# Down projection of a ConvFFN in fp32: the second block group takes six gated tiles in place of four, the plain group between the two takes two in place of four, and three of the seven low parts of its operands move from VectorE to GpSimd

## The chip, the cores and the metric

The kernel runs on one core of a Trainium2 chip. The metric is the device time of one execution in microseconds (us); less is better. Beside the time of several runs there is one execution recorded by the hardware profiler, from which all rows below come.

Six engines appear in the rows. PE (TensorE) multiplies matrices, and PEld is its weight load, which runs beside it. DVE (VectorE) and POOL (GpSimd) do elementwise work, ACT (ScalarE) copies and casts, and SP (SyncE) issues DMA transfers, as POOL does too. Each engine works through its own queue in order and waits for the others by semaphores.

## The reference

The reference is a trunk of two layers over 16 learned meta tokens and 1024 frames (1040 rows) with a model width of 1024. Each layer has a mixing part (gated linear attention and softmax attention) and then a feed-forward part, which is the one that the change touches:

```python
def conv_ffn(x, w_up, conv_w, conv_b, w_down):
    h = x @ w_up
    L = h.shape[1]
    hp = jnp.pad(h, ((0, 0), (CONV_W - 1, 0), (0, 0)))
    hc = conv_b
    for j in range(CONV_W):
        hc = hc + hp[:, j:j + L] * conv_w[j]
    u, g = jnp.split(hc, 2, axis=-1)
    return (jax.nn.silu(g) * u) @ w_down

for i in range(DEPTH):
    ...
    h = h + conv_ffn(rms_norm(h, ffn_norm[i]), w_up[i], conv_w[i], conv_b[i], w_down[i])
return rms_norm(h, final_norm)[:, N_META:]
```

All of it is fp32. The width D_FF of the gated activations, 2816, is 22 tiles of 128.

## The kernel before, in words

**How a product is made.** Activations lie transposed: 128 features on the partitions, the rows of the sequence along the free axis. An fp32 product is three matmuls in the type fp32r (`mm3`): high part by high part, low part of the weight by high part, high part by low part of the activation. A high part is a rounded copy that ACT makes (`split`, L377), a low part is source minus high part, a subtraction with two inputs in SBUF (L378). Weights are split in the same way (`weights`: load, ACT copy to hi, subtraction to lo at L230; `up_split` L1162 and L1163 for weights of the block groups).

**The down projection.** The gated tiles 0 to 21 are written to DRAM (`actd`) by the stage before and loaded again (tag `st`). They are multiplied with the down weights in groups, given by `GROUPS, LAST`, in this order in the program:

- `n` (0, 3): a plain group of tiles 0 to 2. For each of eight output tiles m and two halves of the sequence, one PSUM bank sums 3 tiles; ACT copies it out (L1715) and POOL issues a DMA that adds it to the residual `hm` in DRAM (L1717).
- `s` (3, 8): block group 1 (`down_blocks`). Weights and activations are seen as 2 by 2 blocks (output pairs j, halves of the eight tiles, halves of the sequence), and seven products of sums and differences of blocks (p from 1 to 7) stand for the eight block products. There are 4 x 7 = 28 products (j, p) in the order of `seq`; its last ones are (3,7), (3,2), (3,5), (3,4), (3,3). Product 5 begins PSUM bank p2 and product 3 adds on in the same bank, after the bank has been added to `dg` in between. Outputs gather in SBUF tiles `du` and `dg` (ACT copies L1623, VectorE adds L1622), and `hand_on` sends them to the residual: by an accumulating DMA to `hm` that POOL issues (L1617), or, when the residual is in SBUF, by a VectorE add (L1614).
- `r` (11, 4): a plain group that adds each bank to the residual tile `h0` to `h7` in SBUF (VectorE, L1713). SP loads these tiles from `hm` ahead (L1688). Bank (2m + half) modulo 4 is used, so that four banks are filled in turn.
- `s` (15, 4): block group 2, with the residual in SBUF.
- LAST (19, 3): the last three tiles, in `down_last`.

Layer 0 computes 2 x 520 rows, in two pieces of 260 a half; layer 1 computes 2 x 512, in one piece.

**What sets the order.** PE runs in the order of the program. The other engines' queues are ordered by a scheduler that goes by readiness and estimated durations. `prepare` is a generator that makes the activations for later groups: for a plain group one high part and one low part of a tile (`ah`, `al`, 1040 wide); for a block group the operands x1 to x7 of two tile pairs at a time, out of four loaded blocks (a0, a1, b0, b1, all `st`) and differences of them (`t2` and overwritten `st`, VectorE L1546), each split into hi and lo by `split`, 1040 wide for two tile pairs and 520 wide for one that is left over. `pump` moves this generator forward while free slots are there: all these tiles are slots of one pool of 33 (plus some that other stages lend), and a new tile in a slot waits for the last use of the old one. So the operands of block group 2 are built while block group 1 runs, in the slots that its operands leave.

Of the kernel before, what the change touches and what calls it, by code (L numbers as in the profile page):

```python
# [10 lines left out]
F32 = mybir.dt.float32  # L11
# [3 lines left out]
ALU = mybir.AluOpType  # L15
# [33 lines left out]

GROUPS, LAST = (("n", 0, 3), ("s", 3, 8), ("r", 11, 4), ("s", 15, 4)), (19, 3)
HALVES, HALVES_LAST, HALVES_OUT = (0, 520, 520), (8, 524, 516), (16, 528, 512)
AHEAD = 4
LANDING = 4
# [8 lines left out]
class Slots:  # L64
# [15 lines left out]
    def get(self, dtype, name, shape=(128, T), first=()):  # L80
        id = next((i for i in self.free if i in first), None) or next(i for i in self.free if i not in self.lent)
        self.free.remove(id)
        pool, tag = id
        t = pool.tile(list(shape), dtype, tag=tag, name=name)
        return Slot(t, id)
# [85 lines left out]
class Kern:  # L171
# [199 lines left out]
            self.rsqrt_mean(r, ps[:, :n], y0[:, :n], a[:, :n], nm.pop("pin", False))  # L371
        return r

    def split(self, hi, lo, src, scale=None):
        nc = self.nc
        if scale is None:
            nc.scalar.copy(hi, src)  # L377
            nc.vector.tensor_tensor(out=lo, in0=src, in1=hi.bitcast(F32), op=ALU.subtract)  # L378
        else:
            nc.scalar.mul(hi, src, scale)  # L380
            nc.vector.scalar_tensor_tensor(out=lo, in0=src, scalar=scale, in1=hi.bitcast(F32),
                                           op0=ALU.mult, op1=ALU.subtract)
# [562 lines left out]
    def attention(self, lyr, nm, hsrc, chunks, feed):  # L945
        tc, nc, s = self.tc, self.nc, self.slots
        self.ch, self.ctiles = CH_HEAD[lyr], CT_HEAD[lyr]
        with tc.tile_pool(name=f"aps{lyr}", bufs=2, space=PSUM, reuse_waits="tile") as pp2, \
# [64 lines left out]
            with tc.tile_pool(name=f"att{lyr}", bufs=2, reuse_waits="tile") as ap, \  # L1013
# [5 lines left out]
                def plan(p):  # L1019
# [15 lines left out]
                    elif p == 4:  # L1035
# [15 lines left out]
                        def split(j):  # L1051
# [3 lines left out]
                            for m in range(NSPLIT):  # L1055
                                nc.gpsimd.dma_start(hT[m][:, c0:c0 + n], hsrc[m][:, c0:c0 + n])
                        split(2)
                        boxes[1]["w"] = self.weights(boxes[1]["src"], own)

                        def ev(m):  # L1060
# [3 lines left out]
                            return f  # L1064

                        before = {(1, 2): lambda: split(1), (1, 1): lambda: split(0)}
                        for m, j in [(m, j) for j in (2, 1, 0) for m in (0, 1)] + [(m, j) for m in (2, 3) for j in (2, 1, 0)]:
                            c0, n = chunks[j]
# [407 lines left out]
    def prepare(self, halves, acts, X):  # L1476


        nc, s = self.nc, self.slots
        W = halves[2]  # L1480
        own = slice(halves[0], T)
        get = lambda name, dt=F32: s.get(dt, name, (128, 2, 520))
        ahead = []

        def load_act(j):
            t = s.get(F32, "st")
            nc.sync.dma_start(t[:, own], self.actd[j][:, own])
            return t

        def load(j0, m, h):  # L1490
            t = get("st")
            for i in range(m):
                nc.sync.dma_start(t[:, i, :W], self.actd[j0 + i][:, halves[h]:halves[h] + W])
            return t


        loads = []
        for kind, g0, ng in GROUPS + (("r",) + LAST,):
            if kind != "s":
                loads += [(1, lambda j=j: load_act(j)) for j in range(g0, g0 + ng)]  # L1500
                continue
            nk = ng // 2
            for k0 in range(0, nk, 2):
                m = min(2, nk - k0)
                loads += [(4, lambda j=g0 + k0, m=m, nk=nk: [load(i, m, h) for i in (j, j + nk) for h in range(2)])]
        size = lambda: loads[0][0] if loads else 0

        def fetch():
            if loads:
                ahead.append(loads.pop(0)[1]())  # L1510

        def use():
            return ahead.pop(0)
        for kind, g0, ng in GROUPS + (("r",) + LAST,):
            while len(ahead) < 2 and loads:
                yield size()
                fetch()
            if kind != "s":
                for j in range(g0, g0 + ng):
                    yield 2 + size()  # L1520
                    fetch()
                    t = use()
                    ah, al = s.get(F32R, "ah"), s.get(F32R, "al")
                    hi = nc.scalar.copy(ah[:, own], t[:, own])
                    lo = nc.vector.tensor_tensor(out=al[:, own], in0=t[:, own], in1=ah[:, own].bitcast(F32),
                                                 op=ALU.subtract)
                    if self.among_blocks:
                        self.tc.keep_in_program_order(hi)
                        self.tc.keep_in_program_order(lo)
                    s.put(t)  # L1530
                    acts[j] = (ah, al)
                continue
            nk = ng // 2
            for k0 in range(0, nk, 2):
                m = min(2, nk - k0)

                def put(p, src):

                    hi = get(f"x{p}", F32R)
                    lo = get(f"x{p}", F32R) if m == 2 else hi  # L1540
                    h, l = (hi[:, :m, :W], lo[:, :m, :W]) if m == 2 else (hi[:, 0:1, :W], hi[:, 1:2, :W])
                    self.split(h, l, src[:, :m, :W])
                    X[g0][p].append(([hi, lo] if m == 2 else [hi], h, l))

                def tt(out, a, b, op):
                    nc.vector.tensor_tensor(out=out[:, :m, :W], in0=a[:, :m, :W], in1=b[:, :m, :W], op=op)  # L1546
                yield m
                a0, a1, b0, b1 = use()
                put(1, a0)
                yield m  # L1550
                put(2, b0)
                yield 1 + m
                tt(a1, b1, a1, ALU.subtract)
                t2 = get("t2")
                tt(t2, a1, a0, ALU.add)
                put(6, t2)
                yield m
                tt(a0, b1, t2, ALU.subtract)
                put(5, a0)
                s.put(a0)  # L1560
                yield m
                put(7, a1)
                s.put(a1)
                more = k0 + 2 < nk
                yield m + (size() if more else 0)
                if more:
                    fetch()
                tt(b0, b0, t2, ALU.subtract)
                s.put(t2)
                put(4, b0)  # L1570
                s.put(b0)
                yield m
                put(3, b1)
                s.put(b1)
        yield 99
# [374 lines left out]
```

## Time and profile before

| | |
|---|---|
| time, median of 3 runs | 2472.36 us (2470.87 to 2472.37) |
| the profiled execution | 2473.53 us, span 2471.5 us |
| granted TensorE clock | 0.998 |
| block group 1 (layer 0 / layer 1) | 1038.8 to 1119.8 / 2261.8 to 2340.7 us |
| plain group `r` | 1119.6 to 1165.7 / 2340.5 to 2384.9 us |
| block group 2 | 1165.5 to 1205.9 / 2384.7 to 2423.8 us |
| matmuls in them, layer 0 | 672, 384, 336 |
| matmuls in them, layer 1 | 336, 192, 168 |

The stretches run from the start of the first matmul on the group's activations to the modelled end of the last. Matmuls are pipelined, so a 260 wide one has a duration of 0.28 us in the rows, though one follows the other every 0.12 us. In a row of a group stand the line, the engine, the operation, the tiles written and read (without buffer numbers), the shapes, and the count; behind the bar the busy time, the mean duration in ns, and the idle time before it with what ended it. In a row of the timeline stand the start and the duration in us first; square brackets at the end give idle time before the instruction and what ended it. In the view of TensorE's waits stand the total wait, how often, and the longest.

### The profile page before, as it was taken

The page shows a single profiled execution, that of the slowest core. Times are in us where ns is not written, and L with a number is a line of the kernel's source. Part 1 is how long each engine was busy: PE and PEld are TensorE (multiplying, and loading weights), DVE is VectorE, ACT ScalarE, POOL GpSimd, SP SyncE. Part 2 cuts the span into 40 slices and gives each one's busy share as a digit, 9 for nine tenths or more (in the row PEclk, how much of TensorE's full clock was granted, in tenths as well). Part 3 has the DMA queues.
Part 4 walks back from the last instruction along what each step waited for, and adds up shares of the span by engine and source line. Part 5 has one row for each costly group of instructions (what it writes and reads, how often), then busy time and mean ns, then how long its engine had stood idle before and what let it go on. Part 6 is the DMA issues. An engine that isn't in the chain of part 4 may idle for free.

```text
span 2471.5 us, 47309 instructions
## 1 busy us (share of the span) xinstructions
PE 2440.1 (99%) x18286; PEld 2358.4 (95%) x18286; DVE 1873.4 (76%) x3769; ACT 1318.1 (53%) x2857; POOL 384.9 (16%) x565
## 2 busy tenths in 40 slices
PE   9999999999999999999999999999999999999998
PEld 8999999999999999999999999999999999998887
DVE  8665776869988888855866666777699888887667
ACT  7345766646555555642543456666465555556433
POOL 2023433210000000100220234331100000001002
PEclk9999999999999999999999999999999999999999
DMA  3222134443322224764312222243433212247722
GB/s 131 74 84 76 43 95 130 126 124 104 119 76 83 83 73 144 185 161 140 118 47 74 80 78 71 71 142 108 146 84 116 91 65 90 82 151 184 210 71 88
DMA packets 121680, 260.39 MB, mean 105 GB/s; under 512 B 15248, under 2 KB 37008, under 8 KB 121456
## 3 DMA queue, kind: packets, MB, share of 16 engines
q1 hardware_dynamic: 97008, 182.18, 23.8%
q0 software_dynamic: 22288, 72.81, 10.5%
q8 instruction: 143, 2.34, 0.4%
q10 hardware_dynamic: 2160, 2.38, 0.3%
q14 instruction: 81, 0.66, 0.1%
HBM read 176.74 MB, written 67.80 MB: 99 GB/s over the span
## 4 chain that ended last, share of the span: by engine, by line
PE 48%; issue 31%; DVE 13%; ACT 4%; DMA 2%; POOL 1%; SPq 0%; DVEq 0%; POOLq 0%; ACTq 0%
PE mm L261 7%; PE mm L263 7%; PE mm L262 7%; PE down L262 4%; PE down L261 4%; PE down L263 4%; PE av L780 3%; PE tr L754 2%; PE S L718 1%; DVE x L1188 1%; DVE S L721 1%; PE S L719 1%; ACT P L733 1%; DVE lo L1163 1%; DMA raw<-in_wm_dram 1%
## 5 line engine op out<-in xcount | busy, mean ns | idle before, releaser
L262 PE MATMUL up<-x,lo 128*128 128x260 f32 x2240 | 632.0, 282 | 0.9 <-DVE lo L1163 0.8
L261 PE MATMUL up<-x,hi 128*128 128x260 f32 x2240 | 632.0, 282 | 0.1
L263 PE MATMUL up<-x,hi 128*128 128x260 f32 x2240 | 632.0, 282 | 0.0
L262 PEld LDWEIGHTS up<-x,lo 128*128 128x128 f32 x2240 | 421.9, 188 | 1.4 <-DVE lo L1163 1.3
L261 PEld LDWEIGHTS up<-x,hi 128*128 128x128 f32 x2240 | 421.9, 188 | 0.4 <-ACT hi L1162 0.3
L263 PEld LDWEIGHTS up<-x,hi 128*128 128x128 f32 x2240 | 422.1, 188 | 0.0
L1162 ACT CAST hi<-raw 128x512 fp32r<-128x512 f32 (+1 forms) x490 | 266.3, 553 | 208.5 <-PE up L263 89.6
L261 PE MATMUL mm<-xh,hi 128*128 128x348 f32 (+6 forms) x1056 | 359.8, 341 | 0.0
L1163 DVE TENSOR_TENSOR lo<-raw,hi 128x512 fp32r<-128x512 f32 (+1 forms) x490 | 286.8, 600 | 81.3 <-ACT hi L1162 80.8
L263 PE MATMUL mm<-xl,hi 128*128 128x348 f32 (+6 forms) x1056 | 339.7, 322 | 0.0
L262 PE MATMUL mm<-xh,lo 128*128 128x348 f32 (+6 forms) x1056 | 338.7, 321 | 0.0
L261 PEld LDWEIGHTS mm<-xh,hi 128*128 128x128 f32 x1056 | 199.5, 189 | 2.3 <-issue 1.4
L262 PEld LDWEIGHTS mm<-xh,lo 128*128 128x128 f32 x1056 | 199.4, 189 | 0.3
L263 PEld LDWEIGHTS mm<-xl,hi 128*128 128x128 f32 x1056 | 198.6, 188 | 0.1
L1144 DVE TENSOR_TENSOR raw<-raw,raw 128x512 f32<-128x512 f32 (+1 forms) x230 | 146.8, 648 | 28.9 <-DMA raw<-in_wd_dram 26.3
L733 ACT ACTIVATE P<-S,m 116x460 f32<-116x460 f32 (+2 forms) x224 | 124.9, 562 | 77.1 <-DVE m L721 74.3
L228 ACT CAST hi<-raw 128x512 fp32r<-128x512 f32 (+2 forms) x152 | 87.4, 576 | 140.5 <-PE mm L263 59.6
L262 PE MATMUL down<-x,lo 128*128 128x260 f32 (+1 forms) x504 | 161.2, 320 | 0.6 <-DVE lo L1163 0.6
L263 PE MATMUL down<-x,hi 128*128 128x260 f32 (+1 forms) x504 | 161.2, 320 | 0.0
L261 PE MATMUL down<-x,hi 128*128 128x260 f32 (+1 forms) x504 | 161.1, 320 | 0.0
L378 DVE TENSOR_TENSOR PT<-tr,PT 116x464 fp32r<-116x464 f32 (+3 forms) x240 | 123.1, 515 | 48.9 <-ACT PT L377 47.2
L1424 POOL DMA_DIRECT2D actd<-cv x44 | 23.6, 535 | 734.5 <-DVE cv L1423 734.5
(313 smaller groups left out, 5957.8 us busy)
## 6 DMA issues: line engine op xcount, KB each, us to landing
raw<-in_wm_dram SPq DMA_DIRECT2D x326, 256.0 KB, 3.0
raw<-in_wd_dram SPq DMA_DIRECT2D x48, 256.0 KB, 4.4
actd<-cv POOLq DMA_DIRECT2D x22, 520.0 KB, 3.0
actd<-cv POOLq DMA_DIRECT2D x22, 512.0 KB, 2.9
cb<-cd SPq DMA_DIRECT2D x16, 520.0 KB, 3.9
kA<-kA SPq DMA_DIRECT2D x24, 260.0 KB, 4.0
kL<-kL SPq DMA_DIRECT2D x24, 260.0 KB, 4.7
st<-actd SPq DMA_DIRECT2D x24, 260.0 KB, 3.7
```

The source lines that it names most:

```text
L228: nc.scalar.copy(hi[:, :n, :], raw[:, :n, :])
L261: nc.tensor.matmul(ps, wh, xh[:, c0:c0 + n], start=first, stop=False, skip_group_check=more)
L262: nc.tensor.matmul(ps, wl, xh[:, c0:c0 + n], start=False, stop=False, skip_group_check=more)
L263: nc.tensor.matmul(ps, wh, xl[:, c0:c0 + n], start=False, stop=last, skip_group_check=more)
L378: nc.vector.tensor_tensor(out=lo, in0=src, in1=hi.bitcast(F32), op=ALU.subtract)
L718: nc.tensor.matmul(S[:rows, :n], q["qA"][e][:, qs], q["kA"][e][:, c0:k1], start=True, stop=False)
L733: nc.scalar.activation(P[:rows, :n], S[:rows, :n], AF.Exp, scale=-1.0, bias=m[:rows, nch - 1:nch], accum_out=(den if nch == 1 else d3[:row ...
L754: nc.tensor.transpose(tr[:w, 3 - j, :rows], P[:rows, o:o + w], id_)
L780: nc.tensor.matmul(av[:, a:b], w.rearrange("p a b -> p (a b)"), x, start=(t == ts[0] and part == 0 and i == 0), stop=(t == last and i == 1))
L1144: nc.vector.tensor_tensor(out=q[out][:, :nk, :], in0=q[a][:, :nk, :], in1=q[b][:, :nk, :], op=op)
L1162: nc.scalar.copy(hi[:, :nk, :], src[:, :nk, :])
L1163: nc.vector.tensor_tensor(out=lo[:, :nk, :], in0=src[:, :nk, :], in1=hi[:, :nk, :].bitcast(F32), op=ALU.subtract)
```

## The change

The table of groups gives two tiles to the plain group `r` (11 and 12) and six to block group 2 (13 to 18). `split` can be told an engine for its low part, and `prepare` names GpSimd for operands 2, 4 and 5 of a group of six. Block group 2 thus has three tile pairs a product: operands 1040 wide for the first two pairs and 520 wide for the third.

```diff
-GROUPS, LAST = (("n", 0, 3), ("s", 3, 8), ("r", 11, 4), ("s", 15, 4)), (19, 3)
+GROUPS, LAST = (("n", 0, 3), ("s", 3, 8), ("r", 11, 2), ("s", 13, 6)), (19, 3)
...
-    def split(self, hi, lo, src, scale=None):
+    def split(self, hi, lo, src, scale=None, eng=None):
         nc = self.nc
         if scale is None:
             nc.scalar.copy(hi, src)
-            nc.vector.tensor_tensor(out=lo, in0=src, in1=hi.bitcast(F32), op=ALU.subtract)
+            (eng or nc.vector).tensor_tensor(out=lo, in0=src, in1=hi.bitcast(F32), op=ALU.subtract)
...
-                    self.split(h, l, src[:, :m, :W])
+                    self.split(h, l, src[:, :m, :W], eng=nc.gpsimd if ng == 6 and p in (2, 4, 5) else None)
```

In all, TensorE has 16613 matmul rows where it had 16649.

VectorE at the end of block group 1 in layer 0. `dg` and `du` are the outputs of j = 3, a tile with x and a digit is the low part of that operand of block group 2, `st` and `t2` are its blocks, `lo` is a plain weight's low part, and `h0` is the residual in the plain group. Before:

```order
L1546 TENSOR_TENSOR st_14335<-st_14344,t2_14547 128x1040
L378 TENSOR_TENSOR x6_14550<-t2_14547,x6_14549 128x1040
L1622 TENSOR_TENSOR dg_14440<-down_14490,dg_14440 128x520
L378 TENSOR_TENSOR x5_14581<-st_14335,x5_14580 128x1040
L378 TENSOR_TENSOR x7_14659<-st_14338,x7_14658 128x1040
L1546 TENSOR_TENSOR st_14341<-st_14341,t2_14547 128x1040
L230 TENSOR_TENSOR lo_14587<-raw_14584,hi_14586 128x512
L1622 TENSOR_TENSOR du_14266<-down_14490,du_14266 128x520
L378 TENSOR_TENSOR x4_14664<-st_14341,x4_14663 128x1040
L1713 TENSOR_TENSOR h0_14590<-down_14606,h0_14590 128x520
L378 TENSOR_TENSOR x3_14726<-st_14344,x3_14725 128x1040
L1713 TENSOR_TENSOR h0_14590<-down_14632,h0_14590 128x520
```

And after the change:

```order
L1546 TENSOR_TENSOR st_14268<-st_14268,t2_14515 128x1040
L1622 TENSOR_TENSOR du_14260<-down_14452,du_14260 128x520
L378 TENSOR_TENSOR x7_14579<-st_14265,x7_14578 128x1040
L230 TENSOR_TENSOR lo_14481<-raw_14478,hi_14480 128x256
L378 TENSOR_TENSOR x7_14761<-st_14341,x7_14761 128x520
L1622 TENSOR_TENSOR dg_14440<-down_14488,dg_14440 128x520
L230 TENSOR_TENSOR lo_14585<-raw_14582,hi_14584 128x256
L378 TENSOR_TENSOR x1_14677<-st_14339,x1_14677 128x520
L1622 TENSOR_TENSOR du_14260<-down_14488,du_14260 128x520
L1546 TENSOR_TENSOR t2_14718<-st_14341,st_14339 128x520
L378 TENSOR_TENSOR x3_14640<-st_14271,x3_14639 128x1040
L1713 TENSOR_TENSOR h0_14588<-down_14604,h0_14588 128x520
```

The low parts of x5 and x4 are gone from here, and x2's, which stood a few rows further up; two low parts 520 wide (x7 and x1) and a difference (`t2`) for the third tile pair have come in, and both adds to `h0` now stand behind x3.

POOL's queue in the same place: the accumulating stores of block group 1's outputs. Before:

```order
L1617 DMA hm3_107<-dg_14031 128x1040
L1617 DMA hm2_106<-du_13717 128x1040
L1617 DMA hm5_109<-dg_14303 128x1040
L1617 DMA hm4_108<-du_14067 128x1040
L1617 DMA hm7_111<-dg_14440 128x1040
L1617 DMA hm6_110<-du_14266 128x1040
```

And after the change:

```order
L1617 DMA hm3_107<-dg_14031 128x1040
L1617 DMA hm2_106<-du_13717 128x1040
L1617 DMA hm5_109<-dg_14307 128x1040
L1617 DMA hm4_108<-du_14067 128x1040
L378 TENSOR_TENSOR x2_14485<-st_14268,x2_14484 128x1040
L378 TENSOR_TENSOR x5_14549<-st_14262,x5_14548 128x1040
L378 TENSOR_TENSOR x4_14636<-st_14268,x4_14635 128x1040
L1617 DMA hm7_111<-dg_14440 128x1040
L378 TENSOR_TENSOR x2_14680<-st_14343,x2_14680 128x520
L1617 DMA hm6_110<-du_14260 128x1040
L378 TENSOR_TENSOR x5_14724<-st_14339,x5_14724 128x520
```

Low parts of the operands 2, 5 and 4 stand between the store to hm4 and the store to hm7, and two 520 wide ones behind it.

SP's loads of the residual and of the first weights behind it. Before:

```order
L1688 DMA h2_14594<-hm2_106 128x1040
L1688 DMA h1_14592<-hm1_105 128x1040
L1688 DMA h3_14596<-hm3_107 128x1040
L1688 DMA h4_14598<-hm4_108 128x1040
L1688 DMA h5_14600<-hm5_109 128x1040
L1688 DMA h0_14590<-hm0_104 128x1040
L1487 DMA st_14729<-actd20_132 128x1040
L219 DMA raw_14789<-in_wd_dram 128x512
L1688 DMA h7_14604<-hm7_111 128x1040
L219 DMA raw_14847<-in_wd_dram 128x512
L1487 DMA st_15316<-actd21_133 128x1040
L1688 DMA h6_14602<-hm6_110 128x1040
```

And after the change:

```order
L1688 DMA h0_14588<-hm0_104 128x1040
L1688 DMA h1_14590<-hm1_105 128x1040
L1688 DMA h3_14594<-hm3_107 128x1040
L1688 DMA h4_14596<-hm4_108 128x1040
L1688 DMA h5_14598<-hm5_109 128x1040
L1487 DMA st_14632<-actd19_131 128x1040
L219 DMA raw_14727<-in_wd_dram 128x256
L219 DMA raw_14768<-in_wd_dram 128x256
L1688 DMA h7_14602<-hm7_111 128x1040
L219 DMA raw_14807<-in_wd_dram 128x256
L1688 DMA h2_14592<-hm2_106 128x1040
L1688 DMA h6_14600<-hm6_110 128x1040
```

The load of h2 stood ahead of those of h1 and h3 to h5, and now stands behind the load of h7, next to that of h6; the plain group's weights are 256 wide.

## The prediction

> **What bounds the kernel now.** I read the page's busy times first, then what TensorE waits for, then the stretches of the down projection.
>
> ```profile
> PE 2440.1 (99%) x18286; PEld 2358.4 (95%) x18286; DVE 1873.4 (76%) x3769; ACT 1318.1 (53%) x2857; POOL 384.9 (16%) x565
> ```
>
> ```profile
> PE down L261 <- ACT do L1715: 0.8, 1, 0.8
> PE down L262 <- DVE lo L1163: 0.6, 1, 0.6
> ```
>
> TensorE is busy for 99% of the span and loses 1.4 us to waits in all of the down projection. So a matmul that goes is a gain, and a wait that comes is a loss, both in full. Whether a wait comes hangs on how full the other engines are; windows give that (columns: stretch, length, busy time of PE, PEld, DVE, ACT, POOL with counts, clock, DMA).
>
> ```profile
> 1100.00:1110.00 10.00, 10.00 (x85) 10.00 (x85) 8.22 (x9) 6.96 (x10) 1.70 (x2) 1.00 0.53 119
> 1110.00:1120.00 10.00, 10.00 (x86) 10.00 (x85) 9.79 (x12) 5.78 (x7) 0.86 (x1) 1.00 1.04 358
> 1120.00:1165.00 45.00, 45.00 (x379) 45.00 (x378) 19.92 (x34) 6.01 (x12) 0.85 (x1) 1.00 0.40 120
> 1166.00:1206.00 40.00, 40.00 (x336) 40.00 (x335) 32.08 (x58) 22.27 (x49) 0.00 (x0) 1.00 0.20 57
> 2341.00:2385.00 44.00, 44.00 (x193) 35.92 (x192) 19.83 (x35) 6.00 (x12) 0.86 (x1) 1.00 0.41 117
> 2385.00:2424.00 39.00, 39.00 (x170) 31.62 (x169) 32.14 (x58) 22.43 (x49) 0.00 (x0) 1.00 0.20 57
> ```
>
> In layer 0 block group 1 ends at about 1120, the plain group runs to 1165, block group 2 to 1206; layer 1 has the last two. The place to look at is the end of block 1: VectorE is 98% busy there, because the operands of block 2 are built then. GpSimd does almost nothing.
>
> **The change part by part.**
>
> *Matmuls.* A plain tile costs 8 x 2 x 2 x 3 = 96 matmuls in layer 0 (48 in layer 1, with one piece a half). Two plain tiles go: -192 and -96. Block 2 has 28 products of 3 tile pairs in place of 2, 18 matmuls each in place of 12 (9 for 6): +168 and +84. Net -24 at 40.00/336 = 0.119 us and -12 at 44.00/193 = 0.228: 2.86 + 2.74, so **-5.6 us**.
>
> *Weights.* Hi, lo and combined weights of block 2 become 384 wide where they were 256.
>
> ```profile
> L1163 DVE TENSOR_TENSOR lo<-raw,hi 128x512 fp32r<-128x512 f32 x336 | 226.4, 683 | 62.9 <-ACT hi L1162 62.8
> L1163 DVE TENSOR_TENSOR lo<-raw,hi 128x256 fp32r<-128x256 f32 x154 | 61.5, 418 | 18.4 <-ACT hi L1162 18.0
> ```
>
> Halfway between is 0.55, so 44 instructions (28 low parts, 16 combinations) cost VectorE 44 x 0.13 = 5.8 us more, but block 2 lasts 60 us in place of 40: (32.1 + 5.8)/60 = 0.63 busy. TensorE's longer products hide that; uncovered it would be 5.8 a layer. The plain group's weights shrink. I take nothing for both.
>
> *Low parts on GpSimd.* Three of seven, a 1040 wide and a 520 wide one each, leave VectorE. No such row exists for GpSimd; the nearest are
>
> ```profile
> L230 POOL TENSOR_TENSOR lo<-raw,hi 128x512 fp32r<-128x512 f32 x44 | 56.9, 1300 | 72.3 <-ACT hi L228 72.1
> L898 POOL TENSOR_TENSOR cb<-cb,mask 116x116 f32<-116x116 f32 x128 | 58.3, 456 | 251.9 <-DVE m L721 157.3 <-DMA cb<-cd 54.7 <-PE u L553 20.0
> L378 DVE TENSOR_TENSOR x<-st,x 128x1040 fp32r<-128x1040 f32 x18 | 22.1, 1235 | 8.8 <-DMA hm<-du 6.6 <-ACT x L377 2.2
> ```
>
> (1300 - 456)/396 = 2.13 ns a column gives 1300 + 528 x 2.13 = 2.42 us for 1040; bounds are VectorE's 1.24 and twice 1.30, 2.6. I take 2.42, by the slope. The 520 wide ones follow later, in the plain group, where VectorE is under half busy: nothing.
>
> *What they do to VectorE.* The two engines have run side by side after 1212:
>
> ```profile
> 1212.95 1.06 POOL L355 TENSOR_TENSOR r<-r,sq 128x400 f32<-128x400 f32 x1 [91.29 <-ACT sq L354]
> 1215.71 1.61 POOL L355 TENSOR_TENSOR r<-r,sq 128x400 f32<-128x400 f32 x1 [1.69 <-ACT sq L354]
> ```
>
> ```profile
> 1212.97 0.57 DVE L1792 TENSOR_TENSOR h<-mm,h 128x400 f32<-128x400 f32 x1
> 1213.46 1.10 DVE L230 TENSOR_TENSOR wl<-raw,wl 128x512 fp32r<-128x512 f32 x1
> 1215.72 0.68 DVE L230 TENSOR_TENSOR wl<-raw,wl 128x512 fp32r<-128x512 f32 x1
> 1216.33 0.57 DVE L1792 TENSOR_TENSOR h<-mm,h 128x400 f32<-128x400 f32 x1
> ```
>
> The low part at 1213.46 begins inside GpSimd's 1212.95 to 1214.01 and ends 0.55 after it: it stood until GpSimd was through, then took most of its usual 0.68. At 1215.72 it is the other way: VectorE keeps its 0.68, GpSimd takes 0.55 longer. L1792, which reads PSUM, takes 0.57 in both. So two operations that each read two SBUF tiles take turns, and a GpSimd low part stops VectorE's low parts, t and st operations for 2.4 us. [...] Were it not so here, the sum would be the first rival's.
>
> Now the queue. Before, at the end of block 1 (start, length):
>
> ```profile
> 1114.88 0.69 DVE L1622 TENSOR_TENSOR dg<-down,dg 128x520 f32<-128x520 f32 x1
> ...
> 1119.82 0.70 DVE L1622 TENSOR_TENSOR du<-down,du 128x520 f32<-128x520 f32 x1 [0.21 <-PE down L263]
> ...
> 1123.37 0.70 DVE L1713 TENSOR_TENSOR h<-down,h 128x520 f32<-128x520 f32 x1 [1.69 <-DMA h<-hm]
> 1130.62 1.24 DVE L378 TENSOR_TENSOR x<-st,x 128x1040 fp32r<-128x1040 f32 x1 [6.56 <-DMA hm<-du]
> 1131.78 0.69 DVE L1713 TENSOR_TENSOR h<-down,h 128x520 f32<-128x520 f32 x1
> ```
>
> The last product, (3,3), adds into the bank that dg's add reads, so it can't begin before that add ends. The du add at 1119.82 is released by its end, so it begins one product (24 x 0.119 = 2.9) earlier, at 1116.9; product (3,5), which feeds the add, ends at 1114.0. Free of a lock the add ends at 1114.0 + 0.7 = 1114.7, 2.2 us in time: ahead of it VectorE gives up two low parts (2.3) and takes on x7 twice (1.8). By the order shown with the change, ahead of the add stand t2, st, x6, st, x7, lo and x7's second low part, all of two SBUF inputs, and beside them GpSimd does x2, x5 and x4. If VectorE stands for all three, 3 x 2.42 = 7.3, the add ends at 1122.0 and **TensorE waits 5.0 us**. Bounds: two of them ahead, 2.6; with a turn lost to a wait between the engines, 5.5; none, 0. I take 5.0, since VectorE has no pause there to stand in. Layer 1 has the same order: 5.0 again.
>
> *What they do to the stores.* GpSimd also issues the accumulating stores of dg and du into hm:
>
> ```profile
> 1117.84 0.86 POOL L1617 DMA_DIRECT2D hm<-dg  x1 [9.27 <-ACT dg L1623]
> 1120.82 0.85 POOL L1617 DMA_DIRECT2D hm<-du  x1 [2.12 <-DVE du L1622]
> ```
>
> ```profile
> 1127.24 0.32 SPq L1688 DMA_DIRECT2D h<-hm  x1
> 1130.52 0.32 SPq L1688 DMA_DIRECT2D h<-hm  x1
> ```
>
> ```profile
> 1127.29 1.06 ACT L377 CAST x<-st 128x1040 fp32r<-128x1040 f32 x1 [7.18 <-DMA hm<-dg]
> ```
>
> The load of h7 waits for the first store to land: 1127.24 - 1117.84 = 9.4 us. x3's high part waits for the same landing (its slot was dg's), and on VectorE h0's second add stood behind x3's low part (1131.78; the first ran at 1123.37), where now both do. Before, that delay was free: a plain bank was 24 matmuls, 2.9 us, and four banks 11.5. Now a bank is 12, 1.43, and four banks 5.7. The view of the transfers gives these stores' median time from issue to landing:
>
> ```profile
> hm<-dg POOLq DMA_DIRECT2D x4, 520.0 KB, 6.2
> ```
>
> so 6.2 to 9.4. In the new order hm7's store stands behind GpSimd's x4. With the lock that ends at about 1120.6, the store goes at 1122, lands at 1128.2, x3 takes 1.06 + 1.23, h0's first add 0.7: 1131.2. TensorE, five late, leaves the block at 1124.8 and has four banks to 1130.5: **0.7 more**. In layer 1 x3 stands between h0's two adds, one bank more: 0, bounds 0 and 3.
>
> The h2 load, now behind hm6's store (its slot was du's), comes one bank later and is covered by this wait, or costs up to 1 us.
>
> *Sum.* 2473.53 - 5.6 + 10.0 + 0.7 + 0.5 (half of h2's) = 2479.1. That execution is 1.2 us above the median of the runs shown, 2472.36, so I predict **2478** (its own range 2475 to 2481).
>
> **The rivals.**
>
> 1. *No turns here.* For it: 1040 wide operations on GpSimd stand nowhere in this trace, and VectorE's mix differs. Then dg's add is in time, but hm7's store still stands behind x4, whose operands come free with product (3,4) at 1116.9 and whose low part ends at 1119.3. The store lands at 1125.5, x3 at 1127.8, h0's add at 1128.5; TensorE leaves the block at 1119.8 and is through four banks at 1125.5: 3.0 us. In layer 1, with one bank more, 1.6: 2473.5 - 5.6 + 4.6 - 1.2 = 2471.3. Against it: both rows at 1213 and 1215.
> 2. *All hidden.* Low parts fall into pauses, the stores land early: 2473.5 - 5.6 - 1.2 = 2466.7. For it: VectorE is rid of three times 1.24 + 0.62, 5.6 us a layer, and 1100 to 1110 has pauses of 1.8 us. Against it: 98% in the next ten.
> 3. *Slower still: stores as crowded as before, behind the lock.* The DMA engines are full in 1110 to 1120 (share 1.04). With 9.4 us from 1122, hm7 lands at 1131.4, h0's add ends at 1134.4 against 1130.5: 3.9 in place of 0.7, and 2.5 in layer 1 (one bank of 1.43 less): 2478 + 3.2 + 2.5 = 2483.7. It decides from a landing of 6.2 us up. Against it: later stores find fewer loads in front of them.
>
> That the change does not do as it says is no case: TensorE has 36 rows fewer in the order.
>
> **How the numbers follow.** Chances: forecast 0.46, rival 1 0.24, rival 2 0.18, rival 3 0.12. A measurement of this kernel can tell about 0.2%, 4.9 us, from no change: 2467.4 to 2477.3 is "same". That holds rival 1 and a fifth of the forecast's range, 0.24 + 0.09 = 0.33; faster is rival 2, 0.18; slower is the rest, 0.49. The range 2467 to 2485 leaves out half of rival 2 and half of rival 3, 0.15; it takes in two locks in place of three (2473) and the upper bounds (2481).
>
> **What would show it.** Right: before the last product of block 1 TensorE waits about 5 us for DVE dg L1622, once a layer; GpSimd's L378 take 2.4 us or, in turns with VectorE, up to 3.6; VectorE's L378 and L1546 beside them take 2.4 and more in place of 1.2; hm<-dg goes at its old time plus 4; then the plain group lasts 23 us and block 2 60. Wrong: no lengthened rows (rival 1), a wait for h L1713 in place of dg (1 or 3), no wait at all (2), or waits inside block 2, which I cost at nothing.

## The result, and the profile after

The changed kernel takes **2485.84 us** (median of 6 runs, 2485.10 to 2486.79) where the kernel before takes 2472.36 (6 runs, 2470.64 to 2474.08): ratio 1.0053, 95% interval 1.0043 to 1.0063. It is slower by 13.5 us; 2478 was forecast, and 2485 was the upper end of the range. The profiled execution took 2485.22 us.

The page's busy times after, against those of before: TensorE has 36 matmuls fewer and is still busy 2 us longer.

```profile
PE 2442.2 (98%) x18250; PEld 2359.8 (95%) x18250; DVE 1893.4 (76%) x3775; ACT 1326.0 (53%) x2867; POOL 411.1 (17%) x577
```

What TensorE waits for in the down projection, after (total, times, longest):

```profile
PE down L261 <- DVE dg L1622: 10.9, 3, 4.9
...
PE down L261 <- DVE h L1713: 1.2, 2, 0.9
```

Neither row was there before. The timeline shows the first of the long waits, in layer 0. GpSimd (x2: two low parts without a pause between them):

```profile
1108.33 6.77 POOL L378 TENSOR_TENSOR x<-st,x 128x1040 fp32r<-128x1040 f32 x2
1117.94 2.59 POOL L378 TENSOR_TENSOR x<-st,x 128x1040 fp32r<-128x1040 f32 x1 [2.84 <-ACT x L377]
1122.22 0.88 POOL L1617 DMA_DIRECT2D hm<-dg  x1 [1.68 <-DMA h<-hm]
```

VectorE in the same stretch:

```profile
1108.17 1.24 DVE L1546 TENSOR_TENSOR st<-st,t 128x1040 f32<-128x1040 f32 x1
1109.33 3.48 DVE L378 TENSOR_TENSOR x<-t,x 128x1040 fp32r<-128x1040 f32 x1
1112.74 3.46 DVE L1546 TENSOR_TENSOR st<-st,t 128x1040 f32<-128x1040 f32 x1
1116.12 0.69 DVE L1622 TENSOR_TENSOR du<-down,du 128x520 f32<-128x520 f32 x1
...
1118.22 2.87 DVE L378 TENSOR_TENSOR x<-st,x 128x520 fp32r<-128x520 f32 x1
1121.01 0.69 DVE L1622 TENSOR_TENSOR dg<-down,dg 128x520 f32<-128x520 f32 x1
```

Two operations that take 1.24 us alone take 3.48 and 3.46, and one of 0.69 takes 2.87: one of them for each of GpSimd's three low parts, 2.2 us longer each time. In layer 1, too, three low parts lengthen VectorE's rows, by 6.5 us in all. dg's add, with its PSUM input, keeps its 0.69; it is late because it stands behind them. TensorE then:

```profile
1121.76 0.58 PE L261 MATMUL down<-x,hi 128*128 128x260 f32 x1 [4.81 <-DVE dg L1622]
1122.14 0.42 PE L262 MATMUL down<-x,lo 128*128 128x260 f32 x1
```

That is the forecast wait. (The row's third wait for dg, 1.2 us at 1057.9, is a lead given back: TensorE came to block 1 1.2 us earlier than in the execution before, and there VectorE, which adds to dg, had waited for the same weight load, to 1053.7 in both.) What follows it was not forecast: a matmul of 0.42 us in place of 0.28. The windows behind the wait show why (the column behind the engines is the granted clock):

```profile
1122.00:1124.00 2.00, 2.00 (x10) 2.00 (x11) 0.03 (x1) 0.00 (x0) 0.88 (x1) 0.50 1.03 347
1124.00:1126.00 2.00, 2.00 (x11) 2.00 (x10) 0.70 (x1) 1.16 (x2) 0.21 (x1) 0.50 0.98 170
1126.00:1128.00 2.00, 2.00 (x13) 2.00 (x12) 0.64 (x2) 0.00 (x0) 1.07 (x1) 0.63 0.58 113
1128.00:1130.00 2.00, 2.00 (x19) 2.00 (x18) 1.55 (x3) 0.63 (x1) 0.87 (x1) 1.00 0.49 37
```

For 5.7 us after the wait TensorE is granted half its clock and does 10 or 11 matmuls in 2 us where it does 19 later. The last product of block 1 takes 5.36 us in place of 2.87 in layer 0, and 4.78 in place of 2.78 in layer 1.

For every run below I give the **extra time** of a stage: from its first matmul's start to its last one's, less the number of steps times the median step from one matmul to the next. It holds waits and half clock, but not the matmuls themselves (us, of the one profiled execution):

| run | block 1, layer 0 / 1 | plain group, layer 0 / 1 | profiled execution |
|---|---|---|---|
| before | 0.2 / 0.8 | 0.2 / 0.0 | 2473.53 |
| the change | 8.8 / 7.2 | 1.4 / 0.5 | 2485.22 |
| groups alone | 0.1 / 0.2 | 3.9 / 4.0 | 2475.67 |
| GpSimd alone, old groups | 5.6 / 1.4 | 0.2 / 1.8 | 2478.74 |
| two operands on GpSimd | 2.9 / 3.4 | 4.3 / 5.1 | 2481.80 |
| x4 alone on GpSimd | 0.1 / 1.0 | 5.0 / 3.2 | 2476.60 |
| groups, h2's slot | 0.0 / 0.6 | 4.1 / 2.5 | 2474.55 |
| groups, h2's slot, x3 on GpSimd | 0.0 / 0.2 | 1.8 / 4.0 | 2474.81 |
| groups, GpSimd filling tiles | 0.0 / 0.1 | 3.4 / 5.5 | 2474.08 |
| groups, outputs 6 and 7 kept | 0.0 / 0.4 | 0.1 / 0.0 | 2470.20 |
| the same with the old groups | 0.8 / 0.5 | 0.2 / 0.5 | 2476.80 |
| the change, outputs 6 and 7 kept | 7.4 / 7.9 | 0.0 / 0.0 | 2483.18 |

Extra time in block group 2 is within 0.4 us of nothing in all of them. In the change, extra time grew by 16.7 us; less 5.2 for the matmuls (below) that makes 11.5, and the profiled execution is 11.7 longer. That the two agree so well is partly chance: 1.3 of the 16.7 us are the lead given back.

### The profile page after: what moved, and what is told of

It is laid out like the page before. It is cut to its first block, busy times and chain, and to the rows that moved or that the text cites. A ratio compares the mean times of both kernels' runs of the same rounds, so it can differ in the third digit from the quotient of the medians.

```text
span 2483.4 us, 47306 instructions
## 1 busy us (share of the span) xinstructions
PE 2442.2 (98%) x18250; PEld 2359.8 (95%) x18250; DVE 1893.4 (76%) x3775; ACT 1326.0 (53%) x2867; POOL 411.1 (17%) x577
## 4 chain that ended last, share of the span: by engine, by line
PE 47%; issue 32%; DVE 13%; ACT 4%; DMA 2%; POOL 1%; SPq 0%; DVEq 0%; POOLq 0%; ACTq 0%
PE mm L261 7%; PE mm L263 7%; PE mm L262 7%; PE down L261 4%; PE down L262 4%; PE down L263 4%; PE av L780 3%; PE tr L754 2%; PE S L718 1%; DVE x L1188 1%; DVE S L721 1%; PE S L719 1%; ACT P L733 1%; DVE lo L1163 1%; PE wo L262 1%
## 5 line engine op out<-in xcount | busy, mean ns | idle before, releaser
L1162 ACT CAST hi<-raw 128x512 fp32r<-128x512 f32 (+2 forms) x490 | 272.4, 565 | 194.1 <-PE up L263 90.1
L1163 DVE TENSOR_TENSOR lo<-raw,hi 128x512 fp32r<-128x512 f32 (+2 forms) x490 | 295.7, 617 | 84.6 <-ACT hi L1162 84.1
L261 PE MATMUL down<-x,hi 128*128 128x260 f32 (+1 forms) x588 | 190.1, 323 | 10.9 <-DVE dg L1622 10.9
L262 PE MATMUL down<-x,lo 128*128 128x260 f32 (+1 forms) x588 | 189.7, 323 | 0.0
L263 PE MATMUL down<-x,hi 128*128 128x260 f32 (+1 forms) x588 | 189.7, 323 | 0.0
L1144 DVE TENSOR_TENSOR raw<-raw,raw 128x512 f32<-128x512 f32 (+1 forms) x230 | 152.1, 668 | 30.0 <-DMA raw<-in_wd_dram 27.5
L228 ACT CAST hi<-raw 128x512 fp32r<-128x512 f32 (+3 forms) x152 | 84.0, 553 | 123.7 <-PE mm L263 57.4
```

Of the source, the lines that this page charges most:

```text
L228: nc.scalar.copy(hi[:, :n, :], raw[:, :n, :])
L261: nc.tensor.matmul(ps, wh, xh[:, c0:c0 + n], start=first, stop=False, skip_group_check=more)
L262: nc.tensor.matmul(ps, wl, xh[:, c0:c0 + n], start=False, stop=False, skip_group_check=more)
L263: nc.tensor.matmul(ps, wh, xl[:, c0:c0 + n], start=False, stop=last, skip_group_check=more)
L1144: nc.vector.tensor_tensor(out=q[out][:, :nk, :], in0=q[a][:, :nk, :], in1=q[b][:, :nk, :], op=op)
L1162: nc.scalar.copy(hi[:, :nk, :], src[:, :nk, :])
```

## The experiments

The theory (A): GpSimd's low parts stop VectorE's operations with two SBUF inputs while they run, dg's add stands behind those, and TensorE waits. Its rivals: the groups themselves are at fault (B), and the slow last product is contention, not an effect of the wait (C). The runs below stood beside runs of the kernel before on the same chip (median 2472.89 to 2473.14), and ratios are to those.

**The groups alone.**

```diff
-self.split(h, l, src[:, :m, :W], eng=nc.gpsimd if ng == 6 and p in (2, 4, 5) else None)
+self.split(h, l, src[:, :m, :W], eng=None)
```

> The new groups, with every low part on VectorE. Theory A (the loss is made by GpSimd's low parts, which stop VectorE while they run, so that dg's add is late): no wait of TensorE for DVE dg L1622 above 1 us before the last product of block 1, its rows at full clock, no VectorE L378 or L1546 there above 1.3 us. Left over would be the shorter banks of the plain group against the landing of hm7's store (9.4 us in the trace before): 3 to 5.5 us of waits for DVE h L1713 a layer, so 2473 to 2480 us. Rival B (the new groups are at fault by themselves: weights or order): the waits stay at about 5 us a layer and the time within 3 us of 2486. If nothing is left over: 2466.7.

2479.72 us (2475.67 to 2484.43, 5 runs), 1.0037 (1.0023 to 1.0051). The wait for dg is gone in both layers: A, not B, for these 10 us. But the groups alone are no gain either. The plain group loses 3.9 and 4.0 us, in layer 0 at two places. VectorE there:

```profile
1119.30 0.69 DVE L1713 TENSOR_TENSOR h<-down,h 128x520 f32<-128x520 f32 x1
1124.50 1.24 DVE L378 TENSOR_TENSOR x<-st,x 128x1040 fp32r<-128x1040 f32 x1 [4.50 <-DMA hm<-dg]
1125.66 0.69 DVE L1713 TENSOR_TENSOR h<-down,h 128x520 f32<-128x520 f32 x1
...
1131.91 1.31 DVE L1713 TENSOR_TENSOR h<-down,h 128x520 f32<-128x520 f32 x2 [1.23 <-DMA h<-hm]
```

h0's second add stands behind x3, which stands 4.5 us for the landing of the store of dg; later, h2's adds wait for a load that waits for the store of du. Both hid behind banks of 2.9 us before, and do not behind banks of 1.43.

**GpSimd alone, with the old groups.**

```diff
-(("n", 0, 3), ("s", 3, 8), ("r", 11, 2), ("s", 13, 6)), (19, 3)
+(("n", 0, 3), ("s", 3, 8), ("r", 11, 4), ("s", 15, 4)), (19, 3)
...
-eng=nc.gpsimd if ng == 6 and p in (2, 4, 5) else None
+eng=nc.gpsimd if ng == 4 and p in (2, 4, 5) else None
```

> The old groups (four tiles in the plain group, four in block group 2), with the low parts of x2, x5 and x4 on GpSimd. Theory A: VectorE L378 and L1546 rows of 2.4 to 3.6 us beside GpSimd's; ahead of dg's add stand fewer operations than in the change (t2, st, x6, st), so TensorE waits 1 to 3 us for it, and the time is 2474 to 2480. Rival B: no wait, 2472.

2481.72 us (2478.74 to 2482.19), 1.0033 (1.0020 to 1.0045). In layer 0 TensorE waits 3.5 us for dg and loses 1.5 to half clock behind it; in layer 1 it waits 0.3 us there, and 1.7 in the plain group. A holds in layer 0, above its range (1 to 3 us), as the time is (2474 to 2480); the 0.3 us of layer 1 lie below it, and why is not followed. GpSimd and VectorE there:

```profile
1105.97 3.13 POOL L378 TENSOR_TENSOR x<-st,x 128x1040 fp32r<-128x1040 f32 x1
1112.89 3.24 POOL L378 TENSOR_TENSOR x<-st,x 128x1040 fp32r<-128x1040 f32 x1 [3.80 <-ACT x L377]
```

```profile
1106.73 3.47 DVE L1546 TENSOR_TENSOR t<-st 128x1040 f32<-128x1040 f32 x1
...
1113.75 3.48 DVE L1546 TENSOR_TENSOR st<-st,t 128x1040 f32<-128x1040 f32 x1
1117.15 0.69 DVE L1622 TENSOR_TENSOR dg<-down,dg 128x520 f32<-128x520 f32 x1
```

They take turns: GpSimd waits for the rest of a VectorE operation (3.13 where a later run has 2.43 with nothing to wait for), then VectorE for all of GpSimd's.

**Two operands in place of three, and one.**

```diff
-eng=nc.gpsimd if ng == 6 and p in (2, 4, 5) else None
+eng=nc.gpsimd if ng == 6 and p in (2, 5) else None
```

> As the change, but x4's low parts back on VectorE, behind dg's add in its queue. Theory A: one lock of 2.4 us fewer ahead of dg's add, so TensorE waits 2.0 to 2.9 us for it where the change waits 5.0. What is open is the clock: in the change the last product ran at a granted clock of 0.50 after the wait and cost 2.5 and 2.0 us more. If the clock falls by a bound between 1.2 us (a wait in the change after which it stayed at 1.00) and 4.8, this run tells which side 2 to 2.9 is on: at full clock about 2477, at half clock 2481. Rival C (a slower product is contention and not the wait): the last product still takes 5 us.

2481.80 us (2480.25 to 2484.57), 1.0039 (1.0026 to 1.0052). TensorE waits 2.8 and 2.9 us for dg: one lock of 2.2 fewer than in the change, as A has it. Behind these waits the clock stays at 1.00 and the last product keeps its length, so C falls: the same product, with two low parts on GpSimd, is not slow where the wait before it was shorter. But in the same run a wait of 2.7 us in the plain group did halve the clock (the windows after the two waits):

```profile
1117.00:1120.00 3.00, 3.00 (x26) 3.00 (x27) 1.99 (x3) 1.16 (x2) 1.16 (x2) 1.00 1.02 398
...
1129.00:1131.00 2.00, 2.00 (x12) 2.00 (x11) 2.00 (x5) 0.06 (x1) 0.00 (x0) 0.50 0.66 173
```

So there is no single length between 1.2 and 4.8 us at which the clock falls, which my expectation took for granted (the last section tells the cases apart). Its two times, 2477 and 2481, could not tell either: the 2481.80 came with block 1 at full clock, because the plain group lost 4.3 and 5.1 us.

```diff
-eng=nc.gpsimd if ng == 6 and p in (2, 4, 5) else None
+eng=nc.gpsimd if ng == 6 and p == 4 else None
```

> As the change, but only x4's low parts on GpSimd; x2's and x5's are back on VectorE. By the order, dg's add stands ahead of x4's source st in layer 0, so GpSimd's x4 can't stop anything that dg's add waits behind. Theory A: no wait for dg above 1 us in either layer; hm7's store (layer 0) stands behind x4, and TensorE waits for h L1713 as in the run with the groups alone or up to 3 us more. 2473 to 2483. Rival B: 5 us waits for dg stay.

2476.32 us (2471.01 to 2481.11, 11 runs), 1.0012 (1.0003 to 1.0021). No wait for dg, as expected; the plain group loses 5.0 and 3.2. GpSimd's x4, which stands behind the add in the order of the data, cost nothing at the add (the longest wait for dg is 0.2 us).

**What the plain group waits for.** First h2's load, by giving the late slot to h6, then x3's low part too.

```diff
-for k in range(KD):
-    hT.append(s.get(F32, f"h{k}", first=ids))
+hT.extend([None] * KD)
+for k in (0, 1, 6, 3, 4, 5, 2, 7):
+    hT[k] = s.get(F32, f"h{k}", first=ids)
```

> The run with the groups alone, and h6 takes the slot of the late store in place of h2, so that h2's load waits for no store. In the run with the groups alone the plain group lost 3.9 us a layer: 1.8 (layer 0) and 2.3 us (layer 1) at h0's adds behind x3, 1.9 in layer 0 at h2's add, and 1.7 of half clock in layer 1. Theory A2 (short banks, with x3 and the h2 load behind the landing of the last two stores): the waits at h2 go, those at h0 stay; extra time in the plain group about 2 us in layer 0 and 2 to 4 in layer 1, profiled time 2473 to 2475. Rival (the landings are late as a whole, so that the wait only moves on to h6 or h7): the extra time stays at 3.9 a layer, 2475.7.

2475.93 us (2474.07 to 2480.51, 11 runs), 1.0012 (1.0002 to 1.0021). The wait at h2 is gone; the one behind x3 is 2.5 and 2.3 us, and in layer 0 it now halves the clock, so the extra time there is 4.1, not the 2 expected.

```diff
-self.split(h, l, src[:, :m, :W], eng=None)
+self.split(h, l, src[:, :m, :W], eng=nc.gpsimd if ng == 6 and p == 3 and m == 2 else None)
```

> As the run before, and the 1040 wide low part of x3 alone goes to GpSimd, behind the two stores in its queue, so that h0's adds on VectorE stand behind nothing that waits for a store. Theory A2: neither wait is left, extra time in the plain group under 1 us a layer, and since an add with a PSUM input is not stopped by GpSimd, nothing new comes: 2473 - 5.4 + up to 2 = 2467.5 to 2470, faster than both kernels. Rival: GpSimd's low part makes x3 late for block 2 or stops VectorE's 520 wide ones, and the wait moves into block 2 or stays, 2472 or more.

2474.81 us (2471.38 to 2478.00, 11 runs), 1.0008 (0.9999 to 1.0016). The expectation missed. h0's adds are free now, but the wait moved: on ACT a cast waits until GpSimd's low part of x3 is done, and the high part of a plain weight (L228) behind it comes late, so that VectorE's low part of that weight does too (its row names a load of h, but ACT's L228 ends at 1129.60, just before it starts). GpSimd, ACT and VectorE:

```profile
1126.20 2.43 POOL L378 TENSOR_TENSOR x<-st,x 128x1040 fp32r<-128x1040 f32 x1 [5.27 <-DMA hm<-dg]
```

```profile
1128.67 0.63 ACT L377 CAST x<-st 128x520 fp32r<-128x520 f32 x1 [6.77 <-POOL x L378]
1129.20 0.40 ACT L228 CAST hi<-raw 128x256 fp32r<-128x256 f32 x1
```

```profile
1129.64 0.43 DVE L230 TENSOR_TENSOR lo<-raw,hi 128x256 fp32r<-128x256 f32 x1 [4.56 <-DMA h<-hm]
```

Both layers' waits (1.7 and 2.6 us) come from the landing all the same: each queue that held an instruction waiting for it stood there, VectorE's 4.50 us with the groups alone, here GpSimd's 5.27 and, behind GpSimd's low part, ACT's 6.77.

**GpSimd without reading.** GpSimd fills the tiles that VectorE then writes.

```diff
+if ng == 6 and m == 2 and p in (2, 4, 5):
+    nc.gpsimd.memset(l.bitcast(F32), 0.0)
 self.split(h, l, src[:, :m, :W], eng=None)
```

> The groups alone with all low parts on VectorE, and ahead of each of those for x2, x5 and x4 GpSimd fills the 1040 wide tile with zeros, which VectorE then overwrites: GpSimd works at the same places, but reads nothing. Theory A (turns are taken over reading SBUF): VectorE's rows beside the fills keep 1.24 us. Rival (any GpSimd work stops VectorE's operations with two SBUF inputs): VectorE rows lengthened by up to a fill's length.

One execution, the profiled one: 2474.08 us. GpSimd, then VectorE, in layer 0:

```profile
1104.61 1.27 POOL L1543 MEMSET x<- 128x1040 f32 x1
1106.11 0.97 POOL L1543 MEMSET x<- 128x1040 f32 x1 [0.23 <-PE down L263]
```

```profile
1104.48 1.24 DVE L1548 TENSOR_TENSOR st<-st,t 128x1040 f32<-128x1040 f32 x1
1105.92 1.24 DVE L378 TENSOR_TENSOR x<-st,x 128x1040 fp32r<-128x1040 f32 x1 [0.20 <-POOL x L1543]
```

Both fills run wholly or nearly beside a VectorE operation with two SBUF inputs, and that keeps its 1.24; the third fill of this layer falls into a pause of VectorE. So it is GpSimd's reading that they take turns over here: beside its low parts in the change, which read two SBUF tiles, the same operations took 3.46 and 3.48. The waits in the plain group stay, as with the groups alone.

**The landings taken away.** Outputs 6 and 7 of block group 1 stay where they are, and hm is added to them.

```diff
...
+            elif m >= KD - 2:
+                nc.gpsimd.dma_start(x[:, o0:T], self.hm[m][:, o0:T], accum_op=ALU.add)
+                self.kept[m] = x
             else:
                 nc.gpsimd.dma_start(self.hm[m][:, o0:T], x[:, o0:T], accum_op=ALU.add)
                 going.append((i + LANDING, x))
...
             for k in range(KD):
+                if k in self.kept:
+                    hT.append(self.kept.pop(k))
+                    continue
...
```

> The groups alone, all low parts on VectorE, and the outputs 6 and 7 of block group 1 are not stored to hm: GpSimd's DMA adds hm to them where they lie, and they go on as h6 and h7. So no slot, no load and no operand waits for the landing of those two stores any more. Theory A2 (all of the wait that was left in the plain group came from those landings, first at x3, then at h2, then through the queues of SP and ACT): extra time in the plain group under 0.5 us a layer, none in block 1, profiled time 2473.5 - 5.4 + 0 to 1 = 2468 to 2469, faster than both kernels. Rival (banks of 1.43 us are too short for VectorE's adds by themselves, or the weights come late): 2 us or more a layer stay, with waits for h whose own cause is VectorE's work or the weights.

2470.20 us (2467.43 to 2472.47, 11 runs) against 2473.14: **0.9988** (0.9979 to 0.9997), the only run that beats the kernel before. The profiled execution, 2470.20, is above the 2468 to 2469 that were expected, but nothing is left of the waits, in the plain group and block 2 of either layer:

```profile
1116.80:1139.80 23.00, 23.00 (x193) 23.00 (x193) 22.17 (x40) 8.07 (x17) 0.87 (x1) 1.00 0.73 203
1139.80:1200.00 60.20, 60.20 (x505) 60.20 (x505) 38.52 (x60) 23.69 (x44) 0.00 (x0) 1.00 0.16 44
2339.10:2361.10 22.00, 22.00 (x97) 17.88 (x97) 21.40 (x38) 7.83 (x17) 0.88 (x1) 1.00 0.70 195
2361.10:2419.50 58.40, 58.40 (x254) 47.26 (x253) 39.05 (x62) 23.56 (x44) 0.00 (x0) 1.00 0.17 48
```

From first matmul to last, the two stages of layer 0 take 83.4 us where the kernel before takes 86.1, and 80.6 for 83.1 in layer 1: the matmuls are worth 5.2 us. VectorE is 96% busy in the plain group now, so nothing more fits there. In the median, 2.9 of the 5.2 us arrive. Part of the rest shows in the profiled execution: from the end of block 2 in layer 0 to the start of block 1 in layer 1 it takes 1060.3 us where the execution before takes 1055.9, and in that stretch TensorE is twice granted half its clock for 3.41 us, from 1319.07 and from 1677.47, which the execution before is not. What else is in it stays open.

> The same handling of outputs 6 and 7, with the old groups (four tiles in the plain group, four in block group 2), all on VectorE. The kernel before lost nothing in its plain group (0.2 us), so nothing can be won: 2472 to 2474, within 0.1% of before, and the difference to the run before is what the groups alone are worth, 5.4 us.

2473.73 us (2472.55 to 2476.80, 11 runs), 1.0007 (0.9998 to 1.0015): without the groups this edit is worth nothing, as expected; its profiled execution was its slowest. The difference to the run before is 3.5 us in the medians, not the 5.4 expected.

> The change as it is (low parts of x2, x5 and x4 on GpSimd), with the same handling of outputs 6 and 7. Theory A: the 5 us waits for dg's add and the half clock behind them stay in both layers (extra time in block 1 of 7 to 9 us), and the plain group loses under 1 us: 2481 to 2485. Rival (the wait at dg's add comes from the crowded stores): it shrinks to under 3 us.

2482.28 us (2480.60 to 2483.18, 5 runs), 1.0033 (1.0020 to 1.0046). The waits at dg stay, 4.96 and 5.10 us, and the half clock behind them; the plain group loses nothing. The stores of outputs 6 and 7 have no part in the wait at dg; those of outputs 0 to 5 were left as they were.

## Why the prediction was wrong

**What bounds, and the matmuls.** Right: TensorE sets the time, and the matmuls are worth 5.2 us where 5.6 were reckoned.

**The weights at nothing.** Right: extra time in block 2 is within 0.4 us of nothing in every run.

**GpSimd's 2.42 us for 1040 columns, by the slope of two rows.** Right: 2.43 where it ran without a wait (x3 on GpSimd).

**The turns, and dg's add behind them.** Right in mechanism and place: 5.0 us a layer were forecast, 4.97 and 5.07 came. That the size is so exact is luck in layer 0: the three turns took 6.6 us, not 7.3, and the time to spare was 1.7 us, not 2.2, so that two errors cancel. Rival 1 (no turns) and rival 2 (all hidden) fall with the lengthened rows.

**The price of a wait. This is the step that failed.** It stood at the start: a wait that comes is a loss in full, that is, at its own length. The two waits cost 7.5 and 7.1 us, since the product behind each ran at half clock: 2.5 and 2.0 us more, **4.5 us** that no term of the sum and no rival held. The kernel before had no wait long enough to show it in these stages (its longest in the down projection is 0.8 us). But its trace shows a half clock near the start, which I did not weigh: 0.50 for 3.41 us from 11.06, after a stretch of the same length in which TensorE stood for 1.6 us.

**The stores.** Right about the landing, wrong about where it would be felt. hm7's store went at 1122.22 (1122 forecast), and the load of h7 that waits for it at 1129.05, 6.8 us later (6.2 taken). But the 0.7 us at h0's adds in layer 0 did not come: the half clock kept TensorE in block 1 to 1127.1, not 1124.8, and the adds were done at 1131.6, in time. What came is a wait of 0.9 us at h2's adds: the store of du landed at 1135.19, the load of h2 that waits for it at 1138.94. SP, then VectorE (whose row names TensorE, though h2's first bank was full by 1134.7):

```profile
1135.20 0.80 SPq L1688 DMA_DIRECT2D h<-hm  x2
```

```profile
1139.06 1.31 DVE L1713 TENSOR_TENSOR h<-down,h 128x520 f32<-128x520 f32 x2 [2.05 <-PE down L263]
```

Extra time in the plain group came to 1.7 us more than before, 1.2 forecast; the nearness is luck. So is that of rival 3: its 2483.7 is the forecast nearest to the result, but it took landings of 9.4 us and 6.4 us of waits in the plain groups, and the landing took 6.8.

By the terms as measured: 2473.5 - 5.2 + 10.0 + 4.5 + 1.7 = 2484.5, against 2485.22; the forecast was 2479.1 in the same frame, so 4.5 of the 6.1 us are the clock. The rest is 0.5 in the plain group, 0.4 of the matmuls and 0.7 that lies elsewhere.

**What the forecast did not see behind the first wait.** Rival 1 took the short banks to cost 4.6 us in all without the turns, with low parts still ahead of the stores; they cost 7.9 with the groups alone, of which 1.7 are half clock. In the change the long wait at dg hid most of it: the two losses do not add up, and taking one away bares the other.

**Open.** The groups alone spread over 8.8 us in 5 runs, and the profiled one was the fastest. Its waits of 1.8 to 2.3 us lie where the clock falls in some cases and not in others, which would make such a spread. The mean granted clock of each run agrees in part: it is 0.998 in the two shortest and 0.996 in the three longest, but the second is 3.7 us longer than the first at the same clock. No trace of a longer run shows it.

## What to carry to other kernels

A TensorE wait of some us can cost more than itself: behind all seven waits of 3.1 us and more here the clock was halved, and a half clock cost 1.5 to 2.7 us. Add that before calling a wait small. Moving a 1040 wide operation with two SBUF inputs from a full VectorE to GpSimd freed 1.2 us of VectorE here and stopped it for 2.2 where another with two SBUF inputs was queued; choose operands that stand behind the urgent instruction, or (not tried here) a place where VectorE has pauses. When a stage is shortened, list what its old length hid: here a store's landing that held up four queues in turn, and that was best removed, not rescheduled.

## What the runs showed of the hardware

The clock after a TensorE wait in the down projection, over all runs: after the eight waits of 1.3 to 2.1 us it stayed at full speed; after 2.27, 2.32, 2.51, 2.55 and 2.71 it was halved, and after 2.33, 2.79 and 2.92 it was not; after all seven of 3.1 and more it was halved. The half clock cost 1.5 to 2.7 us a time.

The records of the granted clock tell the cases apart. In each trace all its changes lie on one grid of 3.413 us: in the change it falls at 451.63, 1120.64, 1687.25, 2346.02 and 2475.73 and rises at 455.04, 1127.47, 1690.66 and 2352.85, 1 to 195 whole steps from one change to the next, to 0.01 us. So the half clock behind a wait lasted one or two steps, 3.41 or 6.83 us, of which the first part can lie in the wait. The windows below follow the grid (columns as above: length, then TensorE's busy time; the clock stands behind the engines). First the change, where TensorE stood for a whole step:

```profile
1117.23:1120.64 3.41, 0.00 (x0) 0.00 (x0) 3.41 (x3) 2.39 (x4) 2.59 (x1) 1.00 1.02 417
1120.64:1127.47 6.83, 5.71 (x26) 5.72 (x27) 2.20 (x5) 1.16 (x2) 2.17 (x2) 0.50 0.96 269
1127.47:1130.88 3.41, 3.41 (x30) 3.41 (x29) 2.96 (x4) 1.06 (x2) 0.87 (x1) 1.00 0.44 38
```

Then two operands on GpSimd, where the wait of 2.79 us (2.63 from the end of one row to the start of the next) lies across the line at 1115.33:

```profile
1111.91:1115.33 3.42, 2.32 (x20) 2.11 (x18) 3.42 (x4) 1.76 (x3) 0.48 (x1) 1.00 0.52 173
1115.33:1118.74 3.41, 1.88 (x15) 1.89 (x16) 2.96 (x5) 1.84 (x4) 0.88 (x1) 1.00 1.02 415
1118.74:1122.15 3.41, 3.41 (x31) 3.41 (x30) 2.25 (x3) 1.37 (x3) 2.17 (x2) 1.00 1.04 281
```

It leaves 1.1 us of standing in one step and 1.5 in the next, and the clock stays. Over all runs, in the down projection, the clock fell from full speed behind every step in which TensorE stood for 2.1 us or more, and behind none in which it stood for 1.8 or less; a line of the grid divides the waits of 2.33, 2.79 and 2.92 so that neither side holds more than 1.8. Elsewhere in the kernel idle time alone does not decide: with outputs 6 and 7 kept the clock fell at 1319.07 behind a step with 1.4 us of standing, and in the kernel before 1.7 us in the step from 1676.76 left it at 1.00.
